# A hybrid attention and recurrence layer on one core: the softmax maximum in one-bank chunks behind every key tile, VectorE's order fixed, the first item's maxima made during the last projection step

## The chip, the cores and the metric

One core of a Trainium2 chip. The metric is device microseconds of one execution, the median of several runs. The layer is one program, at a width of 1024.

## The reference

All arithmetic of the reference is fp32. What matters here is the attention of 2048 latent tokens over 2304 keys (256 of context and 2048 latent), with 8 query heads of 64 in 2 groups that share a key and value head, and beside it a gated linear recurrence in both directions over the same tokens:

```python
def latent_attention(qx, kx, vx, kc, vc):
    ...

    def block(q):
        s = jnp.einsum('bqkgd,bnkd->bkgqn', q, keys).astype(jnp.float32) * scale
        p = jax.nn.softmax(s, axis=-1)
        return jnp.einsum('bkgqn,bnkd->bqkgd', p.astype(vals.dtype), vals)
...
        att_x = latent_attention(qx, kx, vx, kc, vc)
        hg_x, hg_c = hgrn2_bidirectional(px[3:], pc[3:], lb_all[l], g_hg[l])
        x = x + mx[2] * (jnp.concatenate([att_x, hg_x], axis=-1) @ w_out[l])
        x = x + mx[5] * swiglu(modulate(rmsnorm(x, g_norm2[l]), mx[3], mx[4]), w_gu[l], w_down[l])
```

## The kernel before

**Items.** The attention is swept in 32 items: for each of the two groups, 16 tiles of 128 queries, with the group's four heads side by side as 512 columns. An item goes over 18 key tiles of 128 keys. For a key tile, `scores` writes the negated scores, 128 keys x 512 queries, into one PSUM bank `s` by two matmuls: L956 with the high parts of key and query (`K`, `qa`), and L957 with the low parts (`KB`, `qb`). Row 64 of `qb` holds the query's maximum and row 64 of `KB` the constant -1, so that the maximum is already taken off. ScalarE makes the exponential `p` of it (L959). `products` multiplies it with the values (`VS`) into `av`, six key tiles at a time and three tiles late (BATCH and LAGT): 12 matmul pairs for the values (L975), and 32 short ones against ones for the sums (L983), for which GpSimd has added two of the three pairs of tiles (`ps`, L966). At an item's end come the reciprocal `li` (L988), the copy `ot` (L990), two matmuls `pb` which spread `li`, the product `oo` (L998) and its store.

**The maximum.** The exact maximum of an item's scores by the high parts has to be known before its first key tile. So during item n the kernel makes the maxima of item n+1: `chunk` multiplies one head's 128 queries with 1024 keys (two matmuls, L927, into a tile `mx` of two banks, of which there is one), and VectorE reduces these 1024 columns to a minimum (L929); a ninth chunk takes the last 256 keys of all four heads (L932, L934). The table CHUNKS says behind which key tile each stands. `maxima` then transposes the result (`pn`, L942), ScalarE copies it (`mr`), and four DMAs write it into row 64 of the next `qb` (L946). The first item's chunks stand ahead of the sweep.

**The recurrence.** It shares the sweep. A unit is 512 tokens of one head, with seven levels; up to two units (lanes) are in work, and every ninth key tile is a round in which each of them goes one level further: matmuls `pa` (L646), VectorE copies them under a mask into `A` (L656), GpSimd makes the next `M` and `C` (L665, L668) and `Q` (L677, L679), ScalarE copies the other halves of `M` and `C` (L671, L672), VectorE reduces the factors `T` (L683). `prepare` begins a unit (M, C, kk, two Q), from `F` and `q`, which `load` brings by DMA. Between rounds the table STEPS gives places 0 to 5 to single steps of the plan: `keys`, `forward`, `chain`, `diagonal`, `output` and, at the place after an output, its `store`.

**Order.** In the sweep the order of TensorE is as written (`manual_schedule`); the other engines' instructions are ordered by the scheduler from a simulated timeline. All DMAs are issued by SyncE, one after the other. PSUM holds three banks `s`, one `av`, two for `mx` and two of tag `h`, which `pa`, `pn`, `pb` and the steps of the recurrence share.

**Ahead of the sweep** the last two projection steps, `jobs_i`, fill 104 us with matmuls, during which most of SBUF still belongs to the projections. Then the pools of the sweep open: K, KB, the first queries, the mask of the levels (seven DMAs, each with a cast by VectorE) and the first unit's F and q come in, and the first item's nine chunks run.

## Time and profile before

| | us |
|---|---|
| runs | 3409.38, 3412.69, 3413.85 |
| median | 3412.69 |
| the profiled execution | 3405.91 |
| its span in the profile | 3404.1 |

Its stages, with the time that each engine is busy in them:

| window (us) | what runs | TensorE | VectorE | ScalarE | GpSimd | clock |
|---|---|---|---|---|---|---|
| 0 to 618 | modulation, norm, projections | 595.94 | 326.47 | 191.96 | 182.52 | 0.99 |
| 618 to 722 | the last two projection steps | 104.00 | 4.92 | 16.92 | 10.70 | 1.00 |
| 722 to 753 | the start of the attention | 12.38 | 16.78 | 3.91 | 5.63 | 0.60 |
| 753 to 1846 | the sweep, with the recurrence | 1014.38 | 568.95 | 492.61 | 668.82 | 0.99 |
| 1846 to 3404 | output projection, feed-forward | 1502.70 | 809.73 | 599.73 | 769.39 | 0.98 |

How to read what follows. The trace records every instruction of one execution; PE is TensorE, PEld its weight loads, DVE VectorE, ACT ScalarE, POOL GpSimd, SP SyncE; L929 is line 929 of the kernel. A group's row names output and input tiles, shapes and count; behind a bar stand busy time and mean nanoseconds, and behind a second bar the time that the engine idled just before, and who ended it. A row of waits names the waiting engine, tile and line, then the releasing one, then total, count and mean in us. A row of the timeline begins with start and duration in us. A row of windows has the stretch, its length, the busy time of PE, PEld, DVE, ACT and POOL with counts, TensorE's granted clock, the DMA engines' busy share and GB/s.

### The profile page before, as it was taken

Reading aid. Unit: us, or ns where it says so; the run is one execution under the profiler, and the core shown is the slowest. Engines: PE = TensorE matmul, PEld = TensorE weight load, DVE = VectorE, ACT = ScalarE, POOL = GpSimd, SP = SyncE. Lnnn points to the kernel's source line nnn. Section 1 sums busy time; section 2 is a strip of 40 time slices with the busy share of each in tenths; the row PEclk is TensorE's granted clock in tenths of the full one; section 3 lists DMA queues with packets and bytes.
Section 4 is the critical chain, followed back from the end, with each engine's and each line's share of the span. In section 5 each row is a group of like instructions: output and inputs, shape, how many; then the busy total and the mean of one; then the engine's idle time right before and its main releaser. Section 6 shows DMA issues by size and latency. Waiting matters only on the chain. (4 is left out here: it accounts for less than half of the span.)

```text
span 3404.1 us, 55496 instructions
## 1 busy us (share of the span) xinstructions
PE 3229.4 (95%) x21212; PEld 2564.9 (75%) x21212; DVE 1726.8 (51%) x2742; ACT 1305.1 (38%) x2559; POOL 1637.1 (48%) x1450
## 2 busy tenths in 40 slices
PE   8999999978999999999999999999989989999998
PEld 5998987966666666666667887788868768888887
DVE  6445555124555455555543557444465753333566
ACT  4322222214444444444433224333344443333444
POOL 4322222105666666666644218677631357666222
PEclk9999999989999999999999999999989999999999
DMA  7244454341011111201105343444475543323754
GB/s 238 89 147 133 140 152 140 95 120 40 25 40 37 55 36 42 63 28 45 32 15 158 129 139 128 161 142 158 157 252 191 182 135 104 102 96 103 251 200 161
DMA packets 364459, 396.75 MB, mean 117 GB/s; under 512 B 30848, under 2 KB 261216, under 8 KB 363808
## 3 DMA queue, kind: packets, MB, share of 16 engines
q1 hardware_dynamic: 364192, 393.20, 35.9%
q8 instruction: 166, 2.72, 0.3%
q14 instruction: 101, 0.83, 0.1%
HBM read 271.90 MB, written 121.13 MB: 115 GB/s over the span
## 5 line engine op out<-in xcount | busy, mean ns | idle before, releaser
L929 DVE TENSOR_REDUCE mn<-mx 128x1 f32<-128x1024 f32 x256 | 312.8, 1222 | 437.8 <-PE mx L927 338.2
L959 ACT ACTIVATE p<-s 128x512 f32<-128x512 f32 x576 | 326.7, 596 | 474.8 <-PE s L957 469.1
L966 POOL TENSOR_TENSOR ps<-p,p 128x1024 f32<-128x1024 f32 x96 | 228.5, 2380 | 287.4 <-ACT p L959 287.4
L975 PE MATMUL av<-p,VS 128*64 128x256 f32 x2304 | 270.6, 384 | 0.0
L956 PE MATMUL s<-qa,K 128*128 128x512 f32 x576 | 251.8, 437 | 0.0
L927 PE MATMUL mx<-K,qa 128*128 128x512 f32 x512 | 183.4, 440 | 60.7 <-DVE mn L929 60.6
L957 PE MATMUL s<-qb,KB 128*128 128x512 f32 x576 | 230.1, 399 | 4.0 <-DMA KB<-s_k 3.2
L975 PEld LDWEIGHTS av<-p,VS 128*64 128x64 f32 x2304 | 158.3, 137 | 89.7 <-issue 18.7
L1494 POOL TENSOR_TENSOR y<-y,yg 128x512 f32<-128x512 f32 x48 | 76.1, 1600 | 283.9 <-DVE yg L1493 280.1
L927 PEld LDWEIGHTS mx<-K,qa 128*128 128x128 f32 x512 | 86.1, 195 | 119.6 <-DVE mn L929 111.5
L1463 DVE TENSOR_TENSOR x<-lr,x 128x512 fp32r<-128x512 f32 x154 | 119.7, 813 | 67.3 <-ACT x L1462 64.3
L1463 DVE TENSOR_TENSOR dl<-lr,dh 128x512 fp32r<-128x512 f32 x154 | 118.6, 809 | 65.3 <-ACT dh L1462 65.3
L956 PEld LDWEIGHTS s<-qa,K 128*128 128x128 f32 x576 | 110.5, 192 | 36.1 <-issue 17.9
L1462 ACT ACTIVATE dh<-lr 128x512 fp32r<-128x512 f32 x154 | 89.4, 623 | 108.6 <-PE pd1A L1517 52.2
L1462 ACT ACTIVATE x<-lr 128x512 fp32r<-128x512 f32 x154 | 90.4, 626 | 94.0 <-PE pd0A L1517 38.5
L343 PE MATMUL f<-hTh,wh 128*128 128x512 f32 (+1 forms) x320 | 121.0, 378 | 5.4 <-ACT ft L372 5.4
L957 PEld LDWEIGHTS s<-qb,KB 128*128 128x128 f32 x576 | 110.9, 193 | 19.6 <-DMA KB<-s_k 3.5
L1324 PE MATMUL pA<-x,A11h 128*128 128x512 f32 x352 | 113.1, 401 | 9.6 <-ACT A11h L1297 7.2
L1517 PE MATMUL pd0A<-x,x 128*128 128x512 f32 x528 | 120.7, 389 | 0.0
L343 PE MATMUL f<-hTh,wl 128*128 128x512 f32 (+1 forms) x320 | 119.0, 372 | 0.0
L343 PE MATMUL f<-hTl,wh 128*128 128x512 f32 (+1 forms) x320 | 118.8, 371 | 0.0
L1324 PE MATMUL pA<-x,A22h 128*128 128x512 f32 x352 | 112.4, 401 | 4.9 <-DVE r L1374 4.9
(345 smaller groups left out, 9112.6 us busy)
## 6 DMA issues: line engine op xcount, KB each, us to landing
w<-in_w_gu_dram SPq DMA_DIRECT2D x88, 512.0 KB
wm<-in_w_mod_dram SPq DMA_DIRECT2D x24, 1024.0 KB
lr<-s_wT SPq DMA_DIRECT2D x88, 256.0 KB
lr<-in_w_down_dram SPq DMA_DIRECT2D x66, 256.0 KB
wq<-in_w_down_dram SPq DMA_DIRECT2D x44, 256.0 KB
s_wT<-wq SPq DMA_DIRECT2D x44, 256.0 KB
lr<-s_hid1S SPq DMA_DIRECT2D x44, 256.0 KB
lr<-s_hid0S SPq DMA_DIRECT2D x44, 256.0 KB
```

Of the source, the lines that this page charges most:

```text
L343: nc.tensor.matmul(pm[:, :n], w[wi][:, k, c0:c0 + P], hT[b][hi][:, k, :], start=(k == 0 and i == 0), stop=(k == KT - 1 and i == 2))
L927: nc.tensor.matmul(s[:, o:o + 512], self.qa[:, h * P:(h + 1) * P], K[:, k0 + o:k0 + o + 512], start=True, stop=True)
L929: nc.vector.tensor_reduce(self.mn[:, h, c % 2:c % 2 + 1], s, axis=AX.X, op=ALU.min)
L956: nc.tensor.matmul(s, KS[self.g][:, ks], self.qa, start=True, stop=False)
L957: nc.tensor.matmul(s, KB[:, ks], self.qb, start=False, stop=True)
L959: nc.scalar.activation(self.pairs[p][:, o:o + 512], s, AF.Exp, scale=-1.0)
L966: nc.gpsimd.tensor_tensor(t, self.pairs[p - 1], self.pairs[p], op=ALU.add)
L975: nc.tensor.matmul(self.av[i * 64:(i + 1) * 64, :256], VS[:, k, self.g * 64:(self.g + 1) * 64], self.pairs[k // 2][:, o:o + 256], start=(k ...
L1324: nc.tensor.matmul(acc, w[wi][:, k, :], x[xi][k], start=(start and k == 0 and i == 0), stop=(stop and k == KH - 1 and i == 2), skip_group_ ...
L1462: nc.scalar.activation(hi, src, AF.Copy)
L1463: nc.vector.tensor_tensor(lo, src, f32v(hi), op=ALU.subtract)
L1517: nc.tensor.matmul(cur[t], l[:, t * P:(t + 1) * P], r, start=(start and j == 0 and f == 0), stop=(stop and j == NHF - 1 and f == 2), skip_ ...
```

## The change

- A chunk is one matmul of 512 columns (or two of 256), with its own reduction. There are 18 to an item, one behind every key tile, from six tiles before the item's predecessor begins; `mx` is two buffers of one bank.
- The order of VectorE in the sweep is as written too, and that of SyncE until the second item begins.
- The first item's maxima are made in the last projection step (`first_maxima`): K and the queries go into the buffers of weights that are no longer needed, the matmuls stand between those of the projection, and the result goes to DRAM and from there into row 64 of the first `qb`.
- The mask comes as int32 by one DMA, without casts.
- KB is three tiles of 768 keys, which are loaded apart for the second group.
- Rounds of the recurrence stand at tiles 8 and 14 of each item, just ahead of the products there, so 6 and 12 tiles apart; they were 9 apart. `store` comes up to three tiles after its output (`flush`, which holds the three lines that stood in `step`). The context's unit is prepared four places after its load, and its `keys` moved by a few places.
- `ot` and `li` are made after the fourth score tile of the next item, ScalarE's copy first (`drain`); before they followed the last products.

```diff
+        def first_maxima():
+
+            k0, kq = (w_pools[(len(steps) - 2) % 2].tile([P, KT, 256], F32R, tag=t, name=f"early{t}")
+                      .rearrange("p k c -> p (k c)") for t in ("wh", "wl"))
+            k1, qa = kq[:, :256], kq[:, 256:768]
+            nc.sync.dma_start(f32v(k0), s_k[0][:, :2048])
+            nc.sync.dma_start(f32v(k1), s_k[0][:, 2048:])
+            for dup in range(2):
+                nc.sync.dma_start(f32v(qa[dup * 64:(dup + 1) * 64, :]), s_q[0][0, 0].rearrange("d h x -> d (h x)"))
+            small = sm.tile([P, 256], F32, tag="macc", name="small", bufs=1)
+            mn = small[:, :20].rearrange("p (h k) -> p h k", k=5)
+            bank = lambda c: ps_q.tile([P, 512], F32R, tag="pq", name=f"mxfirst{c}").bitcast(F32)
+            for h in range(4):
+                for k in range(4):
+                    s = bank(h * 4 + k)
+                    nc.tensor.matmul(s, qa[:, h * P:(h + 1) * P], k0[:, k * 512:(k + 1) * 512], start=True, stop=True)
+                    nc.vector.tensor_reduce(mn[:, h, k:k + 1], s, axis=AX.X, op=ALU.min)
+                    if k % 2:
+                        yield
...
+            neg = small[:, 20:24]
+            nc.vector.tensor_reduce(neg, mn, axis=AX.X, op=ALU.min)
+            yield
+            yield
+            pm = ps_q.tile([P, 512], F32R, tag="pq", name="pnfirst").bitcast(F32)
+            nc.tensor.transpose(pm[:4, :P], neg, ident)
+            mr = kq[:4, 1280:1280 + P]
+            nc.scalar.activation(mr, pm[:4, :P], AF.Copy)
+            nc.sync.dma_start(s_m0, f32v(mr))
+            yield
...
+            if i == len(steps) - 1:
+                early = first_maxima()
             for n, _ in enumerate(f(c, w)):
+                if i == len(steps) - 1 and n > 2:
+                    next(early, 0)
...
-        ps_mx = pool(hst, "ps_mx", 1, PSUM)
+        ps_mx = pool(hst, "ps_mx", 2, PSUM)
...
-        for lv in range(7):
-            mf = up.tile([P, P], F32, tag="kt", name=f"mf{lv}", bufs=3)
-            nc.sync.dma_start(mf, a["k_mask"][:, lv, :])
-            nc.vector.tensor_copy(mask[:, lv, :], mf)
...
-                if self.late is not None:
-                    self.late[0].store(self.late[1])
-                    self.late = None
+                if self.late is not None and (r, j) in self.plan:
+                    self.flush()
...
-                    self.mn = sm.tile([P, 4, 3], F32, tag="mn", name=f"mn{self.nm}")
+                    self.mn = sm.tile([P, 4, 5], F32, tag="mn", name=f"mn{self.nm}")
-                s = ps_mx.tile([P, 1024], F32, tag="x", name=f"mx{self.nm}_{c}")
+                    self.mn = sm.tile([P, 4, 5], F32, tag="mn", name=f"mn{self.nm}")
+                s = ps_mx.tile([P, 512], F32, tag="x", name=f"mx{self.nm}_{c}")
                 K = KS[self.g]
-                if c < 8:
-                    h, k0 = c // 2, c % 2 * 1024
-                    for o in range(0, 1024, 512):
-                        nc.tensor.matmul(s[:, o:o + 512], self.qa[:, h * P:(h + 1) * P], K[:, k0 + o:k0 + o + 512],
-                                         start=True, stop=True)
-                    nc.vector.tensor_reduce(self.mn[:, h, c % 2:c % 2 + 1], s, axis=AX.X, op=ALU.min)
+                if c < 16:
+                    h, k = divmod(c, 4)
+                    nc.tensor.matmul(s, self.qa[:, h * P:(h + 1) * P], K[:, k * 512:(k + 1) * 512],
+                                     start=True, stop=True)
+                    nc.vector.tensor_reduce(self.mn[:, h, k:k + 1], s, axis=AX.X, op=ALU.min)
...
-                nc.tensor.matmul(s, KB[:, ks], self.qb, start=False, stop=True)
+                nc.tensor.matmul(s, KB[k // BATCH][:, k % BATCH * P:(k % BATCH + 1) * P], self.qb,
+                                 start=False, stop=True)
...
-                if k0 + BATCH == NKT:
-                    self.li = op.tile([P, P], F32, tag="li", name=f"li{self.nm}")
-                    nc.vector.reciprocal(self.li, self.av[:, 256:384])
-                    self.ot = op.tile([P, 256], F32, tag="ot", name=f"ot{self.nm}")
-                    nc.scalar.activation(self.ot, self.av[:, :256], AF.Copy)
+
+            def drain(self):
+                self.ot = op.tile([P, 256], F32, tag="ot", name=f"ot{self.nm}")
+                nc.scalar.activation(self.ot, self.av[:, :256], AF.Copy)
+                self.li = op.tile([P, P], F32, tag="li", name=f"li{self.nm}")
+                nc.vector.reciprocal(self.li, self.av[:, 256:384])
...
-        KB = kvp.tile([P, NTOK], F32R, name="KB")
+        KB = [kvp.tile([P, NTOK // 3], F32R, name=f"KB{r}") for r in range(3)]
...
+        def load_kb(g, r):
+            n = NTOK // 3
+            nc.sync.dma_start(f32v(KB[r][:64, :]), s_k[g][:64, r * n:(r + 1) * n])
...
-        CHUNKS = (-3, -1, 0, 2, 3, 5, 7, 9, 11)
...
+        chunks, loads = {}, {}
+        for n in range(1, NIT):
+            for c in range(18):
+                chunks.setdefault(NKT * (n - 1) - 6 + c, []).append((n, c))
...
-        STEPS = {0: 0, 1: 1, 3: 2, 4: 3, 6: 4, 7: 5}
+        STEPS = {0: [(0, 0)], 1: [(0, 1)], 3: [(0, 2)], 4: [(0, 3)], 6: [(0, 4)], 7: [(0, 5)],
+                 9: [(1, 0)], 10: [(1, 1)], 11: [(1, 2)], 12: [(1, 3)], 13: [(1, 4)], 14: [(1, 5)]}
...
-        border.enter_context(tc.manual_schedule(engines={mybir.EngineType.PE}))
+        border.enter_context(tc.manual_schedule(engines={mybir.EngineType.SP, mybir.EngineType.PE, mybir.EngineType.DVE}))
         items[0].load()
         nc.sync.dma_start(f32v(KS[0]), s_k[0])
+        items[1].load()
         items[0].load_low()
-        nc.sync.dma_start(f32v(KB[:64, :]), s_k[0][:64, :])
+        for r in range(3):
+            load_kb(0, r)
+        nc.sync.dma_start(f32v(items[0].qb[64:65, :]), s_m0.rearrange("h t -> (h t)")[None, :])
+        rec.begin(0)
+        nc.sync.dma_start(mask, a["k_mask"])
         nc.sync.dma_start(VS, s_v.rearrange("(t p) v -> p t v", p=P))
-        nc.sync.dma_start(f32v(KS[1]), s_k[1])
-        for c in range(9):
-            items[0].chunk(c)
-        items[0].maxima()
-        for x in sorted(x for x in events if x < 0):
-            for f, args in events.pop(x):
-                f(*args)
-
+        for x in range(-6, 0):
+            for n, c in chunks.pop(x):
+                items[n].chunk(c)
...
+        outputs = {k for k, (f, _) in rec.plan.items() if f == rec.output}
...
-            if x % 9 == 0:
-                rec.begin(x // 9)
...
-            if k == 0 and n == NCH:
-                nc.sync.dma_start(f32v(KB[:64, :]), s_k[1][:64, :])
+            if n == NCH - 1 and k in (8, 14):
+                load_kb(1, k // BATCH - 1)
+            if n == NCH and k == 0:
+                load_kb(1, 2)
+            if x == NKT:
+                nc.sync.dma_start(f32v(KS[1]), s_k[1])
+            if x == NKT:
+                border.close()
+                border.enter_context(tc.manual_schedule(engines={mybir.EngineType.PE, mybir.EngineType.DVE}))
+            if k == 6 and n + 2 < NIT:
+                items[n + 2].load()
+            if k == 4 and n + 1 < NIT:
+                items[n + 1].load_low()
             item.scores(k)
-            j = STEPS.get(x % 9)
-            if j is not None:
-                rec.step(x // 9, j)
+            if k == 3 and n:
+                items[n - 1].drain()
+            for m, c in chunks.pop(x, ()):
+                items[m].chunk(c)
+            if rec.late is not None:
+                wait -= 1
+                if wait <= 0:
+                    rec.flush()
+            made = iter(())
+            for hr, j in STEPS.get(k, ()):
+                hr += 2 * n
+                if j == 0 and hr:
+                    rec.begin(hr)
+                rec.step(hr, j)
+                if (hr, j) in outputs:
+                    wait = 3
                 if j != 5:
                     next(rec.beside, 0)
-            for f, args in events.pop(x, ()):
-                f(*args)
-            made = iter(())
-            if x % 9 == 8:
-                made = rec.round()
-                next(made, 0)
-            if x % BATCH == LAGT - 1 and x >= BATCH:
-                y = x - LAGT + 1 - BATCH
-                items[y // NKT].products(y % NKT)
-            next(made, 0)
+                else:
+                    made = rec.round()
+            if k == 13 and n + 1 < NIT:
+                items[n + 1].maxima()
             if k == 5 and n:
                 items[n - 1].finish(ps_h, "h")
+            pending.append(made)
+            if k % BATCH == LAGT - 1:
+                made = [m for m in pending]
+                pending.clear()
+                for m in made:
+                    next(m, 0)
+                y = x - LAGT + 1 - BATCH
+                if y >= 0:
+                    items[y // NKT].products(y % NKT)
+                for m in made:
+                    next(m, 0)
```

TensorE in the sweep, before, from key tile 15 of an item to the next round (`s` scores, `mx` chunk, `pa` the round; the numbers in a name are query tile, group or key tile, and the buffer):

```order
L956 MATMUL s_0_15_9036<-qa_0_8351,K_7774 128x512
L957 MATMUL s_0_15_9036<-qb_7779,KB 128x512
L927 MATMUL mx_0_0_9043<-K_7774,qa_0_8988 128x512 x2
L956 MATMUL s_0_16_9048<-qa_0_8351,K_7774 128x512
L957 MATMUL s_0_16_9048<-qb_7779,KB 128x512
L956 MATMUL s_0_17_9052<-qa_0_8351,K_7774 128x512
L957 MATMUL s_0_17_9052<-qb_7779,KB 128x512
L927 MATMUL mx_0_1_9056<-K_7774,qa_0_8988 128x512 x2
L646 MATMUL pa_9060<-Q_7982,M_6_8931 64x64 x8
L646 MATMUL pa_9060<-Q_8461,M_3_8942 64x64 x8
```

TensorE in the sweep now, from key tile 14 of an item over the round and a batch of products to key tile 15:

```order
L968 MATMUL mx_0_2_10180<-K_7822,qa_0_10029 128x512
L683 MATMUL pa_10183<-Q_9227,M_5_10102 64x64 x8
L683 MATMUL pa_10183<-Q_9790,M_2_10113 64x64 x8
L1019 MATMUL av_0_10072<-p_0_3_10032,VS 64x256 x4
L1019 MATMUL av_0_10072<-p_0_4_10047,VS 64x256 x4
L1019 MATMUL av_0_10072<-p_0_5_10132,VS 64x256 x4
L1027 MATMUL av_0_10072<-ps_0_4_10127,one_7830 32x128 x8
L1027 MATMUL av_0_10072<-p_0_5_10132,one_7830 32x128 x8
L999 MATMUL s_0_15_10250<-qa_0_9309,K_7822 128x512
L1000 MATMUL s_0_15_10250<-qb_7828,KB_7826 128x512
L968 MATMUL mx_0_3_10256<-K_7822,qa_0_10029 128x512
```

A chunk was two matmuls behind two of three tiles; now one matmul stands behind each, and the round's `pa` moved in front of the products.

VectorE before, in an item's first tiles (`mn` reduces a chunk, `T` are factors of the recurrence, `li` and `oo` belong to the item that has ended):

```order
L929 TENSOR_REDUCE mn_0_9042<-mx_0_2_9111 128x1
L683 TENSOR_REDUCE T_6_10287<-T_5_10113 128x8
L929 TENSOR_REDUCE mn_0_9042<-mx_0_3_9141 128x1
L988 RECIPROCAL li_0_9173<-av_0_8901 128x128
L929 TENSOR_REDUCE mn_0_9042<-mx_0_4_9183 128x1
L929 TENSOR_REDUCE mn_0_9042<-mx_0_5_9203 128x1
L998 TENSOR_TENSOR oo_0_9210<-ot_0_9175,pb_0_9207 128x256
L929 TENSOR_REDUCE mn_0_9042<-mx_0_6_9222 128x1
```

VectorE now, at the same place:

```order
L970 TENSOR_REDUCE mn_0_8730<-mx_0_3_8830 128x1
L970 TENSOR_REDUCE mn_0_8730<-mx_0_4_8838 128x1
L970 TENSOR_REDUCE mn_0_8730<-mx_0_5_8845 128x1
L970 TENSOR_REDUCE mn_0_8730<-mx_0_6_8853 128x1
L970 TENSOR_REDUCE mn_0_8730<-mx_0_7_8860 128x1
L970 TENSOR_REDUCE mn_0_8730<-mx_0_8_8868 128x1
L1035 RECIPROCAL li_0_8907<-av_0_8646 128x128
L970 TENSOR_REDUCE mn_0_8730<-mx_0_9_8909 128x1
L970 TENSOR_REDUCE mn_0_8730<-mx_0_10_8918 128x1
L970 TENSOR_REDUCE mn_0_8730<-mx_0_11_8925 128x1
L1043 TENSOR_TENSOR oo_0_8931<-ot_0_8905,pb_0_8928 128x256
```

Four reductions of this `mn` stood ahead of `li`, two between it and `oo`, and a `T` among the first; now nine stand ahead of `li` and three between it and `oo`, and the `T` have gone.

SyncE's queue before, at the start of the attention (`mf` a seventh of the mask, `V` values of the recurrence):

```order
L588 DMA mf_7759<-in_k_mask_dram 128x128
L605 DMA F_7863<-s_f_62 128x1024
L609 DMA q_7865<-s_hq_58 128x512
L588 DMA mf_7762<-in_k_mask_dram 128x128
L588 DMA mf_7765<-in_k_mask_dram 128x128
```

SyncE's queue now, at the same place (`s_m` holds the first maxima, `ie` is output of the projection):

```order
L1086 DMA qb_7828<-s_m_77 1x512
L396 DMA s_i_67<-ie_16_7735 128x256
L642 DMA F_7860<-s_f_62 128x1024
L396 DMA s_i_67<-ie_17_7763 128x256
L646 DMA q_7862<-s_hq_58 128x512
L1088 DMA mask<-in_k_mask_dram 128x896
L1089 DMA VS<-s_v 128x18x128
L958 DMA qb_7829<-s_q_72 64x512
L953 DMA qa_0_7933<-s_q_72 64x512 x2
L849 DMA V_7997<-s_i_66 128x18x128
```

Before, K, KB and VS stood ahead of these rows. Now F and q stand ahead of the mask and of VS, behind one line of `qb` from DRAM, and the second item's queries (`qb`, `qa`) between VS and V.

51 lines of the change are left out of this document (30 added, 21 removed).

## The prediction

> **What bounds the kernel now.** I read the page first, then the stages by windows, then the waits of the attention sweep alone (753 to 1846 us), then the timeline of one stretch of it and of its beginning.
>
> ```profile
> PE 3229.4 (95%) x21212; PEld 2564.9 (75%) x21212; DVE 1726.8 (51%) x2742; ACT 1305.1 (38%) x2559; POOL 1637.1 (48%) x1450
> ...
> L929 DVE TENSOR_REDUCE mn<-mx 128x1 f32<-128x1024 f32 x256 | 312.8, 1222 | 437.8 <-PE mx L927 338.2
> L959 ACT ACTIVATE p<-s 128x512 f32<-128x512 f32 x576 | 326.7, 596 | 474.8 <-PE s L957 469.1
> ```
> ```profile
> 722.00:753.00 31.00, 12.38 (x28) 5.65 (x26) 16.78 (x20) 3.91 (x7) 5.63 (x5) 0.60 0.49 129
> 753.00:1846.00 1093.00, 1014.38 (x9992) 724.18 (x9993) 568.95 (x793) 492.61 (x1034) 668.82 (x710) 0.99 0.14 42
> ```
>
> TensorE bounds every stage but one. In the sweep the others are busy 52% (DVE), 45% (ACT) and 61% (POOL) of the time. In the 31 us before it TensorE is busy 12.38 us. So two things can be won: TensorE's waits in the sweep, and those 31 us. Who makes it wait in the sweep:
>
> ```profile
> PEld mx L927 <- DVE mn L929: 90.8, 111, 4.0
> PE mx L927 <- DVE mn L929: 44.8, 77, 3.6
> PEld mx L932 <- DVE mn L929: 27.1, 27, 2.2
> PE mx L932 <- DVE mn L929: 15.9, 19, 1.8
> ...
> PEld pn L942 <- DVE neg L937: 9.6, 14, 3.0
> PEld pn L942 <- DVE o L769: 6.4, 6, 1.6
> PEld s L957 <- DMA KB<-s_k: 3.5, 1, 3.5
> ```
>
> Nearly all of it is VectorE, at the maximum's chunks (mx) and at the transpose of their result (pn). PEld rows say how long no weights were loaded, PE rows how long no matmul ran; the loss lies between, since a matmul's shown length (0.40 us) is longer than its pace. One stretch tells where:
>
> ```profile
> 1187.72 0.63 PE L927 MATMUL mx<-K,qa 128*128 128x512 f32 x2
> ...
> 1188.39 1.23 DVE L929 TENSOR_REDUCE mn<-mx 128x1 f32<-128x1024 f32 x1 [5.86 <-PE mx L927]
> ...
> 1188.65 0.39 PE L956 MATMUL s<-qa,K 128*128 128x512 f32 x1
> ...
> 1188.88 0.40 PE L957 MATMUL s<-qb,KB 128*128 128x512 f32 x1
> ...
> 1189.67 0.30 PEld L927 LDWEIGHTS mx<-K,qa 128*128 128x128 f32 x2 [0.83 <-DVE mn L929]
> 1189.67 0.74 PE L927 MATMUL mx<-K,qa 128*128 128x512 f32 x2 [0.39 <-DVE mn L929]
> ```
>
> Matmuls of 512 columns follow each other every 0.23 us (1188.65 to 1188.88). The next chunk was due at 1189.11 and started at 1189.67, just after the reduction (1188.39 + 1.23 = 1189.62): 0.56 us lost where the PEld row counts 0.83, so 0.27 less for each wait. With one buffer the loop is matmuls 0.63, reduction 1.23 and the hand-overs, about 2 us, for two key tiles whose six matmuls need 1.38.
>
> **The change part by part.** The sum is made against the profiled execution's own 3405.9 us (span 3404.1); the median of the runs shown, 3412.7, is 6.8 us above it, and I carry that over.
>
> *The waits at the chunks.* The rows with PEld on mx and pn for DVE hold 133.9 us in 158 waits. Less 0.27 each (43) leaves 91. Beside that the two matmuls of a chunk that waited run slower: on the timeline 0.74 us for the pair against 0.63 above, an estimate of 0.11 x 158 = 17. Together **-108 us**. From below the bound is the PE rows on mx alone, 60.7; from above PEld's 134.
>
> *What takes their place.* A chunk is now one matmul (0.23) and one reduction of 512 columns, of which every key tile has one. The trace has no such reduction from PSUM; nearest is one of 512 elements from SBUF, and at 1024 both kinds take 1.22:
>
> ```profile
> 785.50 0.69 DVE L683 TENSOR_REDUCE T<-F 128x256 f32<-128x512 f32 x1 [0.17 <-DMA F<-s_f]
> ...
> L988 DVE RECIPROCAL li<-av 128x128 f32<-128x128 f32 x32 | 30.6, 955 | 58.5 <-PE av L983 58.5
> ...
> L998 DVE TENSOR_TENSOR oo<-ot,pb x32: 408/410/422, 795.9 to 1860.5; 128x256 f32<-128x256 f32 x32
> ```
>
> So 18 x 0.69 = 12.4 us of DVE an item instead of 9 x 1.222 = 11.0. With two buffers the loop of one buffer (0.40 + 0.69 + hand-over 0.1 = 1.19) fits into the two tiles' 1.38 us: a bare stretch has no wait left. But DVE's 0.69 a tile is then TensorE's 3 x 0.23 exactly, so all else on DVE between two batches of products pushes the chunks back, in an order that is now the program's. Queued there are the reciprocal (0.955, now behind ACT's copy ot) and the product oo (0.41), both in the stretch from tile 3 to 8: 1.37 us an item. Two buffers and the pb matmuls take up more than half of it; I keep 0.6 x 31 = 19. Behind the 16 outputs of the recurrence DVE waits in its order for ACT's square, then for POOL's root; the like wait above (pn for DVE o) was 6.4/6 = 1.07, so 17. The copies under the mask and the T reductions stand behind a batch of products and are hidden by it (3.75 us, below). **+36 us**; bounds 12 (overhang wholly absorbed, most outputs too) and 76 (42 and twice 17).
>
> *The rounds of the recurrence* ran every 9 tiles and now stand at tiles 8 and 14: 6 tiles and 12 apart. Between the pa matmuls of 8 and of 14 lie a batch of products and six tiles:
>
> ```profile
> 1194.92 2.81 PE L975 MATMUL av<-p,VS 128*64 128x256 f32 x24
> ...
> 1198.67 0.19 PEld L956 LDWEIGHTS s<-qa,K 128*128 128x128 f32 x1 [0.20 <-issue]
> ```
> ```profile
> L966 POOL TENSOR_TENSOR ps<-p,p 128x1024 f32<-128x1024 f32 x96 | 228.5, 2380 | 287.4 <-ACT p L959 287.4
> ...
> L665 POOL TENSOR_TENSOR M<-M,T 128x256 f32<-128x256 f32 (+1 forms) x120 | 77.1, 643 | 0.5
> ...
> L668 POOL TENSOR_TENSOR C<-M,T 128x256 f32<-128x256 f32 (+1 forms) x120 | 75.9, 644 | 20.9 <-PE pk L694 20.5
> L679 POOL TENSOR_TENSOR Q<-Q,T 128x256 f32<-128x256 f32 x96 | 66.7, 695 | 0.0
> ...
> L627 POOL TENSOR_TENSOR Q<-q,F 128x512 f32<-128x512 f32 x32 | 40.7, 1292 | 7.5 <-DMA F<-s_f 4.9 <-PE po L756 2.6
> ```
>
> That is 3.75 + 6 x 0.69 = 7.9 us of TensorE. POOL has four Q (2.78), two M and two C (2.57) and one sum ps (2.38): 7.7 us, just inside. Where a new unit starts in the odd half (8 of 16) two Q of L627 come to it, 2.58, and it is 2.4 us late: 19, of which half, since POOL's order also takes these Q earlier: **+10 us**, between 0 and 38 (all 16).
>
> *ACT* needs 0.6 us for an exponential against 0.69 a tile: covered. *KB in three tiles*, each reloaded while the item before still runs, drops the one wait of 3.5: **-3 us**.
>
> *The start.* What happens in the 31 us:
>
> ```profile
> 722.03 0.62 PE L927 MATMUL mx<-K,qa 128*128 128x512 f32 x2
> ...
> 724.05 0.43 SPq L605 DMA_DIRECT2D F<-s_f  x1
> ...
> 728.19 0.67 ACT L616 ACTIVATE M<-F 128x512 f32<-128x512 f32 x1 [5.53 <-DMA F<-s_f]
> ...
> 729.78 0.42 ACT L672 ACTIVATE C<-C 128x256 f32<-128x256 f32 x1
> ...
> 732.48 0.50 PEld L927 LDWEIGHTS mx<-K,qa 128*128 128x128 f32 x2 [5.28 <-DVE mn L929]
> ...
> 748.47 0.17 DVE L937 TENSOR_REDUCE neg<-mn 128x4 f32<-128x12 f32 x1
> ...
> 749.38 1.28 ACT L959 ACT_TABLE_LOAD   x1
> ...
> 754.10 0.60 ACT L959 ACTIVATE p<-s 128x512 f32<-128x512 f32 x1 [3.44 <-PE s L957]
> ```
>
> The first item's nine chunks alternate with DVE, which also waits for mask and F, and the first exponential comes at 754.10. Now these chunks run among the last projection's matmuls: 16 x 0.23 + 4 x 0.12 (256 columns, an estimate at half) = 4.2 us more for TensorE there, so that stage ends at 726.4; their reductions lie on a DVE with nothing else to do. ACT's order still has F's M and C ahead of the exponentials. F is issued as soon as the stage ends, about 726.6; landing takes 728.19 - 724.05 = 4.1; M to C took 2.0 (728.19 to 730.20); the table 1.3. The first exponential then comes at 734.0 instead of 754.1: **-20 us**. Meanwhile TensorE makes six chunks of the second item, paced by DVE, and three score tiles, then waits 2 to 3 us. What is late next: F, q, the mask, VS, then V twice, in this order on SP's queue; VS is needed by the first products, some 13 us after the stage's end. Bounds: 24 gained if F lands a little sooner, 8 if VS is 12 us late.
>
> The mean clock of the 31 us was 0.60. TensorE: Matmul & The Clock Gate, Part 1, of the Trainium skill says that the array drops to half rate after an idle window of about 3.4 us and returns after a busy one; the row agrees. By that rule the new hole could halve the clock of the first tiles for one such window, an estimate of 1.7 to 3.4 us, and the sum below would be some 3330.
>
> Sum: -108 + 36 + 10 - 3 - 20 = **-85 us**: 3321 on the profile's scale, **3327 us** as a median.
>
> **The rivals.** *DVE sets the pace.* Its order is fixed, so the overhang of 1.37 us an item and the waits at the outputs come through whole: 76 in place of 36 gives 3367. For it: DVE and TensorE need the same 0.69 a tile. Against: after each batch DVE starts with an empty queue. Chance 0.13.
>
> *The waits are only cut in two.* If the reductions take more than a tile, TensorE waits at every chunk as before, and the start and KB alone remain: 3412.7 - 23 = 3390. For it: DVE's work for the maximum rises by 1.4 us an item. Against: 1.19 us of loop in 1.38. This would be the change not doing what it is laid out for. Chance 0.10.
>
> *POOL decides, and it is slower.* In the short interval POOL may still have the sum ps of tile 3 before it (another 2.38) and the new unit's kk (1.28, an estimate from L627's size). Then it needs 10.1 us against 7.9 in 24 items and 14.0 in 8: 24 x 2.2 + 8 x 6.1 = 102 instead of 10, and the sum is +7: **3420**. It decides against the change from about 3 us of lateness an item. Against: POOL is 61% busy over the sweep and has the 12-tile interval to catch up. Chance 0.12.
>
> *More is won*: new DVE waits of 12 and none from POOL give 3293. Chance 0.05.
>
> **How the numbers follow.** The forecast has 0.60. Faster needs more than 0.2% (6.8 us, about what a measurement of this kernel tells from no change): 0.60 + 0.13 + 0.05 and 0.06 of the 0.10, 0.84; within it 0.04, the weak end of that last case; slower 0.12. The range takes in the pace rival, the bounds of the new waits and the waits cut in two, and leaves the slower case out: 3290 to 3390.
>
> **What would show it.** Right: DVE's waits of TensorE at mx in the sweep under 40 us together, reductions of about 0.69 us, a usual item of 29 instead of 31.5 us, the first exponential near 734, stages before and after the attention unchanged apart from 4 us in the last projection. Wrong: mx still waiting at most chunks (second rival), DVE without idle time between chunks (first), waits of pa for POOL's Q or M in the tens of us (third), or a hole before the first products.

## The result, and the profile after

| | before | changed |
|---|---|---|
| median of four runs (us) | 3413.3 | 3289.6 |
| lowest to highest | 3409.4 to 3414.2 | 3283.1 to 3298.0 |
| the profiled execution (us) | 3405.9 | 3298.0 |

The ratio is 0.964, with a 95% interval of 0.962 to 0.967: faster by 124 us. The forecast was 3327, and the range began at 3290, so that the median lies 0.4 below its lower end. The direction was right; the gain is half as large again as forecast.

The windows of the changed kernel's profile (columns as in the prediction's rows of windows): the first two hold the last projections and the start of the attention, the third the sweep.

```profile
618.00:728.00 110.00, 110.00 (x885) 107.63 (x884) 18.49 (x26) 19.23 (x44) 9.80 (x14) 1.00 0.27 85
728.00:737.00 9.00, 8.07 (x55) 6.70 (x54) 2.89 (x5) 1.15 (x3) 1.03 (x2) 1.00 0.81 208
737.00:1736.00 999.00, 972.62 (x9993) 725.49 (x9992) 596.01 (x1070) 512.32 (x1039) 674.04 (x715) 0.99 0.18 52
```

TensorE is now busy through the start, too, and 97% of the sweep. Who makes it wait in the sweep, from the view of waits:

```profile
PE s L999 <- ACT p L1003: 11.3, 8, 2.5
PE pn L985 <- DVE o L806: 8.8, 4, 2.2
PE pn L985 <- DVE Sb L776: 2.0, 3, 0.7
PE po L791 <- DVE o L806: 1.6, 1, 1.6
PE mx L968 <- DVE mn L970: 1.6, 3, 0.5
PE pk L731 <- DVE o L806: 0.5, 3, 0.2
...
PEld mx L968 <- DVE mn L970: 15.5, 39, 1.0
...
PEld pa L683 <- POOL M L702: 1.5, 4, 0.8
```

At the chunks 1.6 us are left in the PE rows where 60.7 stood, and 15.5 in the PEld row (0.27 of each of these 39 is no loss). Items that took 31.7 us, the commonest length before, take 28 to 30 now. The largest waits have other owners now: the exponential (p) that score banks wait for, and the recurrence's output (o).

To compare the starts I count from the first matmul of the last projections. First of the kernel before, then of the changed one, from the view of the tile `i` (shortest, median and longest ns, then the first and the last start):

```profile
L350 PE MATMUL i<-wh,hTh x288: 277/283/387, 618.5 to 721.7; 128*128 128x256 f32 x144
```
```profile
L351 PE MATMUL i<-wh,hTh x288: 277/282/387, 626.0 to 733.3; 128*128 128x256 f32 x144
```

From the first to the last it is 103.2 before and 107.3 now, 4.1 more. The changed kernel's stage began 7.5 us late; a run below shows that this was that execution's own. The score matmuls of both, in the same form, give the sweep's beginning and end:

```profile
L956 PE MATMUL s<-qa,K x576: 387/397/775, 752.3 to 1846.0; 128*128 128x512 f32 x192
```
```profile
L999 PE MATMUL s<-qa,K x576: 388/416/776, 737.1 to 1735.7; 128*128 128x512 f32 x192
```

The start itself, in the timeline of the changed kernel:

```profile
737.07 0.40 PE L999 MATMUL s<-qa,K 128*128 128x512 f32 x1
...
737.84 0.67 ACT L653 ACTIVATE M<-F 128x512 f32<-128x512 f32 x1 [3.52 <-DMA F<-s_f]
...
739.86 1.28 ACT L1003 ACT_TABLE_LOAD   x1
...
741.16 2.69 ACT L1003 ACTIVATE p<-s 128x512 f32<-128x512 f32 x5
...
741.81 0.50 PE L999 MATMUL s<-qa,K 128*128 128x512 f32 x1 [2.48 <-ACT p L1003]
```

The first exponential comes 741.2 - 626.0 = 115.2 after that mark, and 754.1 - 618.5 = 135.6 before: 20.4 earlier. The profiled times differ by 107.9, in stages: 7.5 later at the mark, 4.1 more projection, 26.8 less from the last projection matmul to the first score (30.6 to 3.8), 95.1 less in the sweep (first to last score, 1093.7 to 998.6), and 2.4 more behind it.

### The profile page after: what moved, and what is told of

Its sections match the earlier page's. It is cut to its first block, busy times and chain, and to the rows that moved or that the text cites. A ratio compares the mean times of both kernels' runs of the same rounds, so it can differ in the third digit from the quotient of the medians.

```text
span 3296.2 us, 55769 instructions
## 1 busy us (share of the span) xinstructions
PE 3189.5 (97%) x21212; PEld 2570.5 (78%) x21212; DVE 1751.9 (53%) x3023; ACT 1320.9 (40%) x2559; POOL 1636.9 (50%) x1454
## 5 line engine op out<-in xcount | busy, mean ns | idle before, releaser
L970 DVE TENSOR_REDUCE mn<-mx 128x1 f32<-128x512 f32 x496 | 333.7, 684 | 212.8 <-PE mx L968 207.4
L1003 ACT ACTIVATE p<-s 128x512 f32<-128x512 f32 x576 | 337.9, 597 | 168.6 <-PE s L1000 149.1
L999 PE MATMUL s<-qa,K 128*128 128x512 f32 x576 | 254.2, 441 | 11.3 <-ACT p L1003 11.3
L968 PE MATMUL mx<-K,qa 128*128 128x512 f32 x496 | 201.0, 406 | 2.7 <-DVE mn L970 2.4
L968 PEld LDWEIGHTS mx<-K,qa 128*128 128x128 f32 x496 | 93.5, 189 | 41.4 <-DVE mn L970 17.8
```

What stands on the lines that cost most here:

```text
L968: nc.tensor.matmul(s, self.qa[:, h * P:(h + 1) * P], K[:, k * 512:(k + 1) * 512], start=True, stop=True)
L970: nc.vector.tensor_reduce(self.mn[:, h, k:k + 1], s, axis=AX.X, op=ALU.min)
L999: nc.tensor.matmul(s, KS[self.g][:, ks], self.qa, start=True, stop=False)
L1003: nc.scalar.activation(self.pairs[p][:, o:o + 512], s, AF.Exp, scale=-1.0)
```

## The experiments

In this table the sweep is the time from the first to the last score matmul in each profile. Medians of different rows come partly from different chips, and single executions of one kernel lie up to 16 us apart; the sweep of the one kernel that was profiled twice repeats within 1.8 us and is the finer measure. The last column is what half clock can have cost that sweep: half of the time for which the trace's clock records show TensorE at a granted clock of 0.50. Such stretches follow some waits and not others (the section on the start shows when), so they differ between executions. Without them the change and its repetition have the same sweep, 990.1 and 990.0.

| run | median | ratio to before | sweep | half clock |
|---|---|---|---|---|
| before | 3413.3 | | 1093.7 | 15.3 |
| the change | 3289.6 | 0.964 (0.962 to 0.967) | 998.6 | 8.5 |
| changed_again | 3284.7 | 0.964 (0.962 to 0.966) | 996.8 | 6.8 |
| start_late | 3289.2 | 0.965 (0.962 to 0.967) | 990.0 | 2.9 |
| two_banks | 3368.2 | 0.989 (0.986 to 0.991) | 1079.5 | 3.4 |
| dve_free | 3316.4 | 0.973 (0.971 to 0.976) | 1025.0 | 13.8 |
| rounds9 | 3310.1 | 0.971 (0.968 to 0.973) | 1022.6 | 8.5 |
| one_buffer | 3487.7 | 1.024 (1.023 to 1.026) | 1196.2 | 7.8 |
| b_banks | 3348.0 | 0.983 (0.981 to 0.985) | 1043.7 | 12.1 |
| act_first | 3293.3 | 0.968 (0.966 to 0.969) | 1004.1 | 10.2 |
| pn_bank | 3277.2 | 0.963 (0.961 to 0.965) | 987.4 | 1.7 |
| dve_plus | 3290.3 | 0.964 (0.962 to 0.967) | 999.7 | 3.4 |
| ctx_slow | 3284.1 | 0.963 (0.961 to 0.965) | 996.0 | 5.1 |
| together | 3283.3 | 0.963 (0.961 to 0.965) | 988.7 | 3.4 |

**The chunks: two_banks, one_buffer, b_banks.**

```diff
-        ps_mx = pool(hst, "ps_mx", 2, PSUM)
+        ps_mx = pool(hst, "ps_mx", 1, PSUM)
...
+                s = ps_mx.tile([P, 1024], F32, tag="x", name=f"mx{self.nm}_{c}")
...
+            for c, x in enumerate((-3, -1, 0, 2, 3, 5, 7, 9, 11)):
+                chunks.setdefault(NKT * (n - 1) + x, []).append((n, c))
```

> The changed kernel with the chunks of before: two banks, one buffer, nine an item, at the old places; VectorE's order stays fixed, the rounds and the start stay. Theory (the chunks' size and the second buffer took the waits away): TensorE's waits for VectorE at mx come back, some 100 us in the sweep, and the time is 80 to 115 us longer, near 3390. Rival (VectorE's fixed order took them away): less than 20 us longer.

The sweep is 81 us longer, the low end of what the theory expected (the median is 79 longer, 3368 and not near 3390), and the view of waits has the old owner back:

```profile
PEld mx L969 <- DVE mn L971: 100.5, 117, 1.7
...
PEld mx L974 <- DVE mn L971: 11.4, 16, 0.8
```

The theory holds. All other parts of the change, with the old chunks, win 14 us of the sweep (1093.7 to 1079.5), and up to 12 of these are half clock (15.3 to 3.4).

```diff
-        ps_mx = pool(hst, "ps_mx", 2, PSUM)
+        ps_mx = pool(hst, "ps_mx", 1, PSUM)
```

> The changed kernel with a single one-bank buffer for mx instead of two; nothing else. Theory (the loop of one buffer is a matmul's 0.40, the reduction's 0.68 and hand-overs, about 1.15 us a tile, against three matmuls of 0.23 = 0.69): each chunk that doesn't follow a batch of products waits some 0.45 us, about 14 an item over 31 items, 195 us longer; range 150 to 230. Rival (the small chunk alone did it, because its reduction of 0.68 is just covered by a tile's matmuls): less than 50 us longer.

The sweep is 198 us longer than the changed kernel's, at 195 expected. Its timeline shows the loop of one buffer:

```profile
797.67 0.50 PE L968 MATMUL mx<-K,qa 128*128 128x512 f32 x1 [0.32 <-DVE mn L970]
...
798.20 0.69 DVE L970 TENSOR_REDUCE mn<-mx 128x1 f32<-128x512 f32 x1 [0.59 <-PE mx L968]
...
798.95 0.50 PE L968 MATMUL mx<-K,qa 128*128 128x512 f32 x1 [0.32 <-DVE mn L970]
```

A chunk every 1.28 us (797.67 to 798.95), where a tile needs 0.69. So the small chunk with one buffer is worse than the old one: the second buffer is what makes it pay.

```diff
-        ps_mx = pool(hst, "ps_mx", 1, PSUM)
+        ps_mx = pool(hst, "ps_mx", 2, PSUM)
...
-                at(NKT * (n - 1) - 6, it.load)
+                at(NKT * (n - 1) - 12, it.load)
...
-                for c, x in enumerate(CHUNKS):
-                    at(NKT * (n - 1) + x, it.chunk, c)
+                for c in range(18):
+                    at(NKT * (n - 1) - 5 + c, it.chunk, c)
```

> The kernel before with one part alone: one-bank chunks in two buffers, 18 an item, one behind every key tile from five tiles before its item's predecessor (and the queries loaded six tiles earlier); VectorE's order stays with the scheduler, the rounds stay nine tiles apart, the first item's chunks stay ahead of the sweep. Theory (the chunks alone carry most of the gain, and a round at tile 17 and a free order give some of it back): the sweep is 45 to 70 us shorter than before, the time near 3345. Rival (without the fixed order and the moved rounds the chunks gain little): less than 25 us shorter in the sweep.

The sweep is 50 us shorter than before, as the theory had it. 50 by the chunks alone and 14 by the rest alone make 64 of 95: the remaining 31 come only from both together. Without the half clock it is 47 and 2 of 88, so that 39 come only from both.

**The order and the rounds: dve_free, rounds9.**

```diff
-        border.enter_context(tc.manual_schedule(engines={mybir.EngineType.SP, mybir.EngineType.PE, mybir.EngineType.DVE}))
+        border.enter_context(tc.manual_schedule(engines={mybir.EngineType.SP, mybir.EngineType.PE}))
...
-                border.enter_context(tc.manual_schedule(engines={mybir.EngineType.PE, mybir.EngineType.DVE}))
+                border.enter_context(tc.manual_schedule(engines={mybir.EngineType.PE}))
```

> The changed kernel with VectorE's order in the sweep given back to the scheduler; all else stays. Theory (two buffers are enough, the order matters little): the sweep changes by less than 8 us. Rival (the fixed order carries the gain, since a reduction behind something that waits holds up the next chunk): 30 us longer or more, with TensorE's waits at mx for VectorE back in tens of us.

The sweep is 26 us longer: the order matters much, between what theory and rival said and nearer to the rival. One place in its timeline shows why:

```profile
764.22 1.22 DVE L720 TENSOR_REDUCE T<-F 128x512 f32<-128x1024 f32 x1 [2.54 <-DMA F<-s_f]
765.35 0.95 DVE L720 TENSOR_REDUCE T<-T 128x16 f32<-128x32 f32 x4
766.22 0.95 DVE L1035 RECIPROCAL li<-av 128x128 f32<-128x128 f32 x1
767.08 0.63 DVE L970 TENSOR_REDUCE mn<-mx 128x1 f32<-128x512 f32 x1
```

The scheduler put a T, whose input F was still under way, ahead of a chunk's reduction. VectorE stood still for 2.54 us, then did 3 us of other work. TensorE had filled both banks shortly ahead of 764.2 and waited 3.47 us for one. Over this sweep its waits for VectorE at mx sum to some 25 us in the PE rows, where the fixed order leaves less than 2.

```diff
-                 9: [(1, 0)], 10: [(1, 1)], 11: [(1, 2)], 12: [(1, 3)], 13: [(1, 4)], 14: [(1, 5)]}
+                 9: [(1, 0)], 10: [(1, 1)], 12: [(1, 2)], 13: [(1, 3)], 15: [(1, 4)], 16: [(1, 5)]}
...
+            if k == NKT - 1:
+                for m in pending * 2:
+                    next(m, 0)
+                pending.clear()
```

> The changed kernel with the recurrence's rounds nine tiles apart as before, at tiles 8 and 17; the one at 17 has no products behind its pa. Theory (a round's copies on VectorE must lie beside a batch of products): two copies of about 0.6 us and the reduction T push the chunks after tile 17 back by 1 to 1.5 us an item, 30 to 45 us, less up to 15 that GpSimd's longer interval gives back: 20 to 40 us longer. Rival (the short interval of six tiles makes GpSimd late and that is what the remaining waits are): 10 to 30 us shorter.

24 us longer, within what the theory expected: VectorE's copies of a round belong beside a batch of products. What GpSimd's longer interval gives back can't be told from this run. The waits for the exponential fall from 11.3 to 2.4 us, but dve_free and two_banks, with the short interval and a slower TensorE, have nearly none either.

**VectorE's reserve: dve_plus.** The extra reductions' results are read by nobody.

```diff
+                junk = sm.tile([P, 1], F32, tag="junk", name=f"junk{self.nm}_{c}")
+                nc.vector.tensor_reduce(junk, f32v(self.qa[:, :64]), axis=AX.X, op=ALU.min)
```

> The changed kernel with a small extra reduction on VectorE (64 columns from SBUF, an estimate of 0.1 to 0.15 us) behind the reduction of each of the 558 chunks of the sweep: 56 to 84 us more work for VectorE. Theory (VectorE has no reserve between two batches, where it needs 0.68 us a tile and TensorE 0.69; it has some beside each batch): about half of it comes through, 25 to 50 us longer. Rival (the two buffers and the batches still take it up, so VectorE is not near setting the pace): less than 12 us longer.

The group of the added instructions, and a stretch of this run's timeline:

```profile
L979 DVE TENSOR_REDUCE junk<-qa 128x1 f32<-128x64 f32 x547 | 114.3, 209 | 0.0
```
```profile
800.75 0.69 DVE L970 TENSOR_REDUCE mn<-mx 128x1 f32<-128x512 f32 x1 [1.83 <-PE mx L968]
801.36 0.21 DVE L979 TENSOR_REDUCE junk<-qa 128x1 f32<-128x64 f32 x1
801.48 0.68 DVE L976 TENSOR_REDUCE mn<-mx 128x2 f32<-128x512 f32 x1
```

547 instructions with 114 us of shown time cost the sweep 1 to 3 us, or some 6 without the half clock (996.3 against 990.0): the rival, less than 12, holds. The rows tell why. The next instruction starts 0.61 after the reduction's start, before its shown 0.69 are over, and the one after that 0.12 later. A reduction of 512 columns takes VectorE 0.6 of the 0.69 us of a tile, not all of it. With the added one it is 0.73, just over a tile; the two buffers and the batches take up most of that.

**The start: start_late, act_first.**

```diff
-                early = first_maxima()
+                early = iter(())
...
+        for c in range(18):
+            items[0].chunk(c)
+        items[0].maxima()
```

> The changed kernel without the early maxima: the first item's 18 one-bank chunks run after the projections, ahead of the sweep, and its maxima take the old way through four DMAs. Everything else stays. Theory (the early maxima are what shortened the start): VectorE needs 18 x 0.69 = 12.4 us for the chunks and the way of the maxima back some 4 us, so the sweep begins 15 to 17 us later than in the changed kernel, and the time is that much longer, about 3305. Rival (the start became short by the mask's one DMA without casts and by the order of SyncE's queue): the sweep begins less than 5 us later.

Between the two. From this run's mark,

```profile
L351 PE MATMUL i<-wh,hTh x288: 277/283/387, 615.8 to 719.0; 128*128 128x256 f32 x144
```
```profile
738.28 0.60 ACT L1003 ACTIVATE p<-s 128x512 f32<-128x512 f32 x1 [3.53 <-PE s L1000]
```

the first exponential comes 122.5 us later, 7.3 behind the changed kernel's and 13.1 ahead of the kernel before. So of the 20 us at the start the early maxima bring 7; with the 18 chunks still there, 13 come from what this run shares with the change at the start. The run b_banks tells part of it: it has the old start but for the two small buffers, and its first exponential comes 128.3 after its mark (746.8 - 618.5), 7 ahead of the kernel before. The other 6 (a mask without casts, the orders of VectorE and SyncE) were not taken apart. The 7 do not show in its median; its runs spread by 14. In its profile the rest of the sweep was shorter by 5.4, mostly by what the next lines show.

A wait of TensorE costs more than itself. These are windows of the changed kernel around the wait at 738.9 to 741.8, and around one of 2 us near 1219:

```profile
738.90:741.80 2.90, 0.42 (x2) 0.01 (x1) 1.15 (x2) 2.84 (x6) 2.90 (x4) 1.00 1.00 329
741.80:743.20 1.40, 1.39 (x6) 1.20 (x7) 0.41 (x1) 1.40 (x3) 1.40 (x3) 1.00 1.03 290
743.20:746.90 3.70, 3.70 (x11) 2.87 (x10) 2.36 (x4) 1.83 (x5) 3.44 (x2) 0.54 1.07 192
746.90:750.00 3.10, 3.10 (x26) 1.96 (x26) 1.38 (x2) 1.18 (x2) 0.00 (x0) 1.00 1.19 261
```
```profile
1219.70:1221.20 1.50, 1.46 (x8) 1.29 (x9) 0.46 (x1) 1.50 (x5) 1.50 (x3) 0.98 0.80 240
1221.20:1224.40 3.20, 3.20 (x12) 2.09 (x10) 0.99 (x3) 3.20 (x8) 3.06 (x4) 0.50 0.04 13
```

The granted clock falls to half, only some 1.5 us after the wait is over. From 743.27 to 746.67 eight matmuls of 512 columns take 3.40 us where they need 8 x 0.23: that costs another 1.6. It doesn't follow every wait, and the trace's clock records show when it does. In the sweep of the changed kernel the clock is 0.50 five times, for 3.4 us each, from 743.3, 1221.1, 1251.9, 1477.1 and 1699.0 on. The last four begin 140, 149, 215 and 280 times 3.413 us behind the first: the clock goes by steps of that length. In the step ahead of each of the five TensorE stood still for 1.95 to 2.24 us in all; in every other step it was 1.62 or less. A wait of 2.23 us that ends at 1024.5 lies across two steps, and no half clock followed. (In all profiles here a step of the sweep at full clock was always followed by half clock if it held 1.9 us or more of this, and never if it held less than 1.65.) So where a wait of some 2 us falls in its step is chance: the item that begins at 1219.7 took 40.2 us here, 37.1 in start_late, 38.6 in changed_again.

```diff
-        border.enter_context(tc.manual_schedule(engines={mybir.EngineType.SP, mybir.EngineType.PE, mybir.EngineType.DVE}))
+        border.enter_context(tc.manual_schedule(engines={mybir.EngineType.SP, mybir.EngineType.PE, mybir.EngineType.DVE, mybir.EngineType.Activation}))
```

> The changed kernel with ScalarE's order as written too, but for the first item alone. Its first exponentials then stand ahead of the M and C of the first unit, which wait for F. Theory (the first exponential is held up by ScalarE's order, not by its scores): it comes 3 to 4 us earlier, TensorE's hole of 2.9 us at the third score tile goes, and with it the stretch at half clock behind it; the first item takes 21.5 to 23 us instead of 26.2, the time is 3 to 5 us shorter. Rival (the table load or the scores' bank hold it): less than 1 us.

A miss. The first exponential did come 3.5 us earlier (111.7 after the mark), but the first item took 35.3 us instead of 26.2. Its waits, 725 to 770 us:

```profile
PE av L1019 <- DMA VS<-s_v: 4.4, 1, 4.4
PEld pd L670 <- POOL kk L662: 4.4, 1, 4.4
```

What comes earlier has VS late, and the first unit's M, written at tile 10, now runs there, so that GpSimd's kk and TensorE's diagonal (pd) are late. Two stretches of 6.8 us at half clock go with these waits. The scheduler's order had M early, and that was worth more than the exponentials.

**The waits that are left: pn_bank, ctx_slow, together.** The place of one wait of pn in the changed kernel's timeline:

```profile
1245.41 2.57 POOL L664 TENSOR_TENSOR Q<-q,F 128x512 f32<-128x512 f32 x2 [0.85 <-PE po L793]
...
1249.46 0.23 POOL L799 TENSOR_SCALAR rs_o<-rs_o 128x4 f32<-128x4 f32 x1
...
1249.73 0.69 DVE L806 TENSOR_TENSOR o<-po,rs_o 128x512 f32<-128x512 f32 x1 [1.64 <-POOL rs_o L799]
...
1250.56 0.27 PE L985 MATMUL pn<-identr,neg 128*4 128x128 f32 x1 [2.25 <-DVE o L806]
```

`neg` was long ready. pn wants the bank of tag h that `po` holds until VectorE's store has read it; that waits for GpSimd's root, which stands behind two Q.

```diff
-                pm = ps_h.tile([P, 512], F32, tag="h", name=f"pn{self.nm}")
+                pm = ps.tile([P, 512], F32, tag=tag, name=f"pn{self.nm}")
...
-                items[n + 1].maxima()
+                items[n + 1].maxima(*((ps_st, "s") if any(r // 2 == n for r, _ in outputs) else (ps_h, "h")))
```

> The changed kernel with pn in one of the three score banks instead of a bank of tag h, in those items in which an output of the recurrence is made. Theory (pn waits for the bank that po still holds until VectorE's store, which waits for GpSimd's root): the five waits of about 2.4 us and the three of 0.7 go, and the half-clock stretches behind them, 10 to 17 us shorter. Rival (the next tile of tag h, pa or psb, waits for the same bank instead): the waits show up at pa or psb, less than 5 us shorter.

11.2 us off the sweep of the change's profile, 9.4 off that of changed_again; without the half clock it is 4.4 and 4.3 (985.7). Where pn waited, pa now waits, but less:

```profile
PE pa L683 <- DVE o L806: 4.0, 3, 1.3
```

Both theory and rival had a part: the wait is shorter by the tile that lies between pn and pa, and no stretch at half clock followed it in this run. The four items with outputs take 36.1, 36.1, 36.1 and 35.9 us here, 37.0, 40.2, 38.6 and 39.7 in the change's profile.

```diff
                 for _ in range(7):
                     c.level()
                     yield
+                    yield
```

> The changed kernel with the levels of the context's unit at every second place of the plan instead of every place; the same instructions, spread over twice the tiles. Theory (TensorE's waits for the exponential, some 14 us in the items with such a unit, come from its copies on ScalarE, which stand ahead of exponentials and wait for GpSimd, that is crowded there): these waits shrink to under 6 us, the sweep is 6 to 12 us shorter. Rival (the four buffers of M and C, which three units then share for longer, are what they wait for): as long as now or longer.

A miss: the sweep is the changed kernel's, and the waits of s stayed, so the spreading did nothing. (The row leaves out the hole at the start; with it 10.4 us stand against 11.3.)

```profile
PE s L1000 <- ACT p L1004: 7.7, 7, 1.6
```

Last, four small edits at once: the bank of pn, a fifth buffer of M, an early exponential of one column, and VS ahead of the mask.

```diff
-                M = up.tile([P, 512], F32, tag="M", name=f"M{h}{u}_0", bufs=4)
+                M = up.tile([P, 512], F32, tag="M", name=f"M{h}{u}_0", bufs=5)
...
+        warm = kvp.tile([P, 1], F32, name="warm")
+        nc.scalar.activation(warm, one32[:, :1], AF.Exp)
```

> The changed kernel with four small edits: pn in a score bank in the items with outputs (as in the run pn_bank), five buffers of M instead of four, one exponential of a single column ahead of the sweep so that ScalarE's table is loaded early, and VS ahead of the mask on SyncE's queue. Theory (the remaining waits are: pn for po's bank, exponentials queued on ScalarE behind a new unit's M that waits for a buffer which GpSimd still reads, and the table load at the start): pn's waits go as in pn_bank (7 to 11 us), the waits of s for the exponential of 0.8 to 2 us go (8 us), the first exponential comes 1.3 us earlier: 16 to 24 us shorter in the sweep than the changed kernel's 998.6, about 978. Rival (what is queued ahead is not held by the buffer but by GpSimd's own lateness): the waits of s stay within 2 us of 11, and the sweep is near pn_bank's 987.

The rival holds for M: the waits of s stay (without the one at the start 7.7 us, and 8.8 in the changed kernel), and the sweep is pn_bank's. The early table load works: the first item takes 23.0 us instead of 26.2, since a wait of 0.90 us instead of 2.48 brings no half clock. The timeline of `together` shows what the exponentials stand behind at one place:

```profile
1215.03 1.31 POOL L705 TENSOR_TENSOR C<-M,T 128x256 f32<-128x256 f32 x2
...
1215.79 0.31 ACT L708 ACTIVATE M<-C 128x128 f32<-128x128 f32 x1 [1.77 <-POOL C L705]
...
1216.13 0.66 ACT L655 ACTIVATE C<-F 128x512 f32<-128x512 f32 x1
...
1216.70 1.07 ACT L1003 ACTIVATE p<-s 128x512 f32<-128x512 f32 x2
```

ScalarE's copy of a level waits 1.77 us for GpSimd's C, and the exponentials are queued behind it. It is not the only way. The changed kernel has seven such waits behind the start. Three of them (5.2 of the 8.8 us) stand behind copies that wait for GpSimd's M. Three others (2.3 us) stand behind the first M of the context's unit, for which ScalarE waited on the transfer of F:

```profile
1186.97 0.43 ACT L653 ACTIVATE M<-F 128x256 f32<-128x256 f32 x1 [5.65 <-DMA F<-s_f]
...
1188.24 0.58 ACT L1003 ACTIVATE p<-s 128x512 f32<-128x512 f32 x1
...
1188.87 0.50 PE L999 MATMUL s<-qa,K 128*128 128x512 f32 x1 [0.78 <-ACT p L1003]
```

pn_bank and together both lie below the change in the median (3277 and 3283), but their intervals overlap with its: by the sweep they are 8 to 11 us better, 4 to 5 of it beside the half clock; by the times that is not proved. Taking GpSimd's root or ScalarE's copies out of these queues, or loading F earlier, was not tried.

> The changed kernel itself once more, on the same chip as the run together. Theory (the 7.5 us by which the last projections began later in its profile than before came from that execution, not from the change): they begin within 4 us of 618 here, the sweep takes 995 to 999 us as before, and the median is near 3290. Rival (the change makes the stages ahead longer): they begin near 626 again.

The mark is at 616.9 here:

```profile
L351 PE MATMUL i<-wh,hTh x288: 277/282/387, 616.9 to 724.3; 128*128 128x256 f32 x144
```

So the 7.5 us ahead of the attention come from the execution and not from the change (the other kernels made from the changed one have the mark between 614.1 and 626.9), and the sweep repeats within 1.8.

## Why the prediction came out as it did

**The waits at the chunks, -108.** Right in place and nearly in size. The sweep fell by 95.1, the new waits (PE rows above) sum to 25.8, and the wait for KB is gone (3.5): 95.1 + 25.8 - 3.5 leaves some 117. Up to 7 of it is half clock (15.3 to 8.5), for which the sum had no term, and some 110 are left for the old waits, their slow matmuls and what is smaller, beside the 108 taken. This is a remainder and was not measured by itself. That the chunk's form and second buffer do it, two_banks and one_buffer show.

**New waits of VectorE, +36.** Mis-sized: the PE rows with DVE hold 14.5. The step that failed is "DVE's 0.69 a tile is then TensorE's 3 x 0.23 exactly": it took the shown length of a reduction for its pace. dve_plus shows 0.6 a tile, and 0.12 more on every tile cost the sweep some 6 us at most. So the overhang of `li` and `oo`, put at 19, left 1.6 at mx. The waits at outputs, put at 17, are 12.9 (pn, po, pk), at the place named, but by another way: not a reduction late behind them, but a PSUM bank.

**GpSimd, +10, and ScalarE, 0.** pa waits for GpSimd in four places, 1.5 us in PEld's row, so the way that was priced at 10 costs next to nothing. But GpSimd's lateness reaches TensorE by two other ways: through VectorE's store into pn (above), and through ScalarE's copies into the exponentials. "ACT needs 0.6 us for an exponential against 0.69 a tile: covered" counted ScalarE's work and not what it waits for, which is GpSimd's M in three places and the transfer of F in three others. Here +10 and 0 stand against 8.8 (the other 2.5 of the 11.3 are the hole at the start); the sum of all new waits is 26 in place of 46.

**KB, -3**, came as put. **The start, -20**: the first exponential is 20.4 earlier and the projection 4.1 longer (4.2 put). The reason was half right: start_late gives the early maxima 7 of the 20, and b_banks the two small buffers another 7, which the prediction gave no part in the start. The order on ScalarE (M, C, table, exponential) was read right, and so was the hole of 2 to 3 us after the third score. That the total came out as put is in part luck.

**The half clock.** The prediction weighed a rule of the Trainium skill (TensorE: Matmul & The Clock Gate, Part 1: half rate after an idle window of about 3.4 us) for the hole at the start. Half clock came there and cost some 1.6 us, but behind a wait of 2.5 us, and elsewhere behind waits of some 2 us; here the measurement decides, and a window need not be idle from end to end. That page of the Trainium skill also says that the window runs freely, and the steps of 3.413 us above agree. The sum had no term for half clock in the rest of the sweep, and it is up to 7 us of the gain.

**The rivals.** "DVE sets the pace" falls with dve_plus, "the waits are only cut in two" with the waits at mx, "POOL decides" with the 1.5 us that pa waits for GpSimd, where tens were its sign. "More is won", 3293, with few new DVE waits and none of pa for GpSimd, is nearest to what happened, and had 0.05.

**From profile to median.** 6.8 us were carried over from the kernel before. The changed kernel's profiled execution lies 8.4 above its median instead, 7.5 of them ahead of the attention. Of the 37.4 us between forecast and median 15.2 are this. On the profile's scale 3321 stands against 3298.0: 30 more won in the sweep (95.1 for 65), and the 7.5 at the mark the other way.

## What to carry to other kernels

With two buffers a small step needs only its engine's pace to stay below the consumer's; with one, the whole loop counts, and halving the step can make it worse. Take an engine's pace from the distance of starts in a stretch without waits, not from shown lengths. When an engine is called covered, look at what stands ahead in its queue and at who holds the PSUM bank: most of the waits that remain came from there.

## What was not expected of the hardware

VectorE begins an instruction some 0.08 us before the one ahead has ended in the records (0.61 after its start, at a length of 0.69), so that 114 us of added shown time cost 1 to 3, or 6 without the half clock. The Trainium skill (VectorE: DVE Perf Modes, The DRAIN you can't avoid) says that the next operation doesn't start until the pipe is empty, but earlier where nothing holds it; these rows agree with the second. And TensorE's clock goes by steps of 3.413 us: with TensorE standing still for 1.9 us or more of one step, the next ran at a granted clock of 0.50, so that two waits of the same length, 2.23 and 2.24 us, cost differently (none behind the one that ends at 1024.5, 3.4 us at half clock behind the one that ends at 1476.3).
